# A two-layer hybrid decoder: layer A's memory projection behind four more value pieces, one gate block moved into its attention, one value tile in another PSUM bank, and the variances of the norms given priority

## The chip, the cores and the metric

The kernel runs on one core of one Trainium2 chip. The metric is the device time of one execution in microseconds (us). TensorE (PE) does the matrix products, VectorE (DVE) and ScalarE (ACT) the elementwise work, GpSimd (POOL) a few small powers, and SyncE (SP) issues nearly all DMAs. Each engine works through its own instructions in a fixed order and waits on semaphores for the others.

## The reference

512 tokens of width 1024 go through two layers. Layer A mixes with a chunked spatial gating beside an attention over 256 memory rows; layer B mixes with a forgetting attention beside a memory attention. Each layer ends in a SiLU feed-forward of width 2816.

```python
def reference(x, mem, ...):
    h = x
    for layer in range(DEPTH):                                   # 2
        a = rmsnorm(h, ln_mix_pre[layer])
        mem_n = rmsnorm(mem, ln_mem[layer])
        if layer < N_A_LAYERS:                                   # layer A
            proj = a @ w_in_a[layer]
            u, v, q_mem = proj[..., :768], proj[..., 768:1536], proj[..., 1536:]
            main = chunked_spatial_gating(u, v, ...)             # gelu(u) * (tril(w_s) @ layernorm(gelu(v)) + b_s)
        else:                                                    # layer B
            ...
            main = forgetting_attention(q, k_s, v_s, log_f_s)
        mixed = jnp.concatenate([main, memory_attention(q_mem, mem_n, w_mem_kv[layer])], axis=-1)
        h = h + rmsnorm(mixed @ w_out[layer], ln_mix_post[layer])
        f = rmsnorm(h, ln_ffn_pre[layer])
        f = (jax.nn.silu(f @ w_ffn_gate[layer]) * (f @ w_ffn_up[layer])) @ w_ffn_down[layer]
        h = h + rmsnorm(f, ln_ffn_post[layer])
    return h
```

## The kernel before

**Products in parts.** Every fp32 operand is cut in two parts: ScalarE rounds it to `hi` (a CAST at L241, or an ACTIVATE with a gain at L245), VectorE takes `lo` as what is left (L241, L246). `mm3` (L193 to L195) makes one product of three matmuls, hi by hi, lo by hi and hi by lo. Weights arrive by DMA in 128x1024 pieces (`raw`, four buffers in turn) and are cut into 128x512 pairs (`whi`, `wlo`, eight buffers), so a piece of weights can't be cut before an older pair was used for the last time.

**Order.** The code is written in one sequence. The framework's scheduler then sets the order on each engine from that sequence, the dependences and priorities; `tc.high_priority()` raises what is written under it. PSUM has three `mm`, three `lg` and two `tr` banks.

**Layer A, in the order written (`layer_a`).** The two query blocks are computed into one `mm` and one `lg` bank (`outs`) while the tokens arrive. Then come *value blocks* 0 to 2 (`value_block`): each is 8 *pieces* of 12 matmuls (128x256 out); two pieces fill one tile `v` for 128 tokens, which ScalarE evacuates into `vg`, scaled by the norm's factor `r4` (L617). The list `fill` holds the 24 pieces, and `pieces(n)` issues the next n. Between them stand:

- the norm of the tokens, `pre` (class `Norm`): `finish` sums squares over partitions with 1-wide matmuls into `st` (L290), adds eps on VectorE into `var` (L292), and takes the power -1/2 on GpSimd into `r` (L262); `spread` transposes `r` into a bank `rb` (L259) and copies it to `rbc` (L305). All scaled evacuations wait for that.
- the norm of the memory, with the same steps, into `rmem`; the parts `mparts` of the memory rows (`mem_inputs`); the cut of the key weights (`mem_key_weights`); and then `mem_project`: two key tiles of 24 matmuls (named `ps`) and two value tiles (`memv`).

Eight pieces are issued ahead of `mem_project`. The memory attention (`attend`, four heads) then has four pieces in each head. After it stand the gelus of `vg` (L663), the LayerNorm statistics, and the *gate blocks* (`gate_inputs`, 24 matmuls 128x512 each, named `ps`): three of them, then the spatial products `s` (L717) by turns with the other three, then the output projection.

**The other norms.** `Norm.finish` is used by the norm at each of three boundaries too (`boundary`, class `PairNorm`): into the feed-forward of layer A, into layer B, and into the feed-forward of layer B, twice each, for the two halves of the tokens. There residuals `h` (L826), squares `sq` (L317, L320) and parts `xslo` stand around it on VectorE.

Of the kernel before, what the change touches and what calls it, by code (L numbers as in the profile page):

```python
# [15 lines left out]
P = 128  # L16
T = 512
D = 1024
KT = 8
TB = T // P  # L20
NMEM = 256
# [5 lines left out]
RMS_EPS = 1e-6  # L27
# [13 lines left out]
def hybrid(ctx: ExitStack, tc: tile.TileContext, i: dict, out: bass.AP):  # L41
# [28 lines left out]
    def small(s, n=4, dt=F32):  # L70
        return sp.tile([P, n], dt, tag=f"s{n}", name=name(s))

    def ps(tag, shape=(P, T), s="ps"):
        return pp.tile(list(shape), F32, tag=tag, name=name(s), bufs=2 if tag == "tr" else 3)

    V, A, PE, G = nc.vector, nc.scalar, nc.tensor, nc.gpsimd
# [24 lines left out]
    def gain(block, k):  # L101
        c = block * KT + k
        return gains[:, c : c + 1]
# [5 lines left out]
                    fill=0.0, base=0, channel_multiplier=-1)  # L109
# [3 lines left out]
                    fill=0.0, base=0, channel_multiplier=-1)  # L113
# [6 lines left out]
                    fill=NEG, base=0, channel_multiplier=1)  # L120
# [28 lines left out]
    def prepared(src, shape, eng=None):  # L149

        raw = wp.tile([P, 1024], F32, tag="raw", name=name("raw"), bufs=4)
        n = shape[0] * shape[1]
        dst = raw[:, :n].rearrange("p (a b) -> p a b", a=src.shape[1]) if len(src.shape) == 3 else raw[:, :n]
        last_load[0] = nc.sync.dma_start(dst, src)
        return weight_parts(raw, shape, eng)

    def weight_parts(raw, shape, eng=None):
        n = shape[0] * shape[1]
        parts = []
        for d in range(0, n, 512):  # L160
            pair = pair_of_parts(min(512, n - d))
            split(raw[:, d : min(d + 512, n)], *pair, eng)
            parts += cut(pair, shape[1])
        return parts
# [26 lines left out]
    def mm3(o, w, x, start, stop, more=False):  # L191

        PE.matmul(o, w[0], x[0], start=start, stop=False, skip_group_check=more)  # L193
        PE.matmul(o, w[0], x[1], start=False, stop=False, skip_group_check=more)  # L194
        return PE.matmul(o, w[1], x[0], start=False, stop=stop, skip_group_check=more)  # L195
# [20 lines left out]
    def queue(blocks):  # L216

        fs, loads = [], {}
        for load, some in blocks:
            loads.setdefault(max(len(fs) - 3, 0), []).append(load)  # L220
            fs += some

        def run(n):
            for f in (*loads.get(n, ()), fs[n]):
                f()

        return [lambda n=n: run(n) for n in range(len(fs))]

    def take(pieces, n):
        some = pieces[:n]  # L230
        del pieces[:n]
        return some
# [10 lines left out]
    def scaled_parts(src, g, hi, lo):  # L243

        last_parts[:] = (A.activation(hi, src, AF.Copy, scale=g),  # L245
                         V.scalar_tensor_tensor(out=lo, in0=src, scalar=g, in1=hi, op0=ALU.mult, op1=ALU.subtract))  # L246
# [14 lines left out]
    def rsqrt(dst, src, n):  # L261
        G.tensor_tensor(out=dst, in0=src, in1=mhalf[:, :n], op=ALU.pow)  # L262

    class Norm:
# [16 lines left out]
        def finish(self, cols):  # L281

            c0, c1 = cols
            tbs = range(c0 // P, c1 // P)
            t0, t1 = c0 // P, c1 // P
            st = ps("tr", (P, 4), s="st")
            for tb in tbs:
                some = self.sums(tb, cols)
                for n, sq in enumerate(some):
                    PE.matmul(st[:, tb : tb + 1], sq, avg, start=n == 0, stop=n == len(some) - 1)  # L290
            v = small("var")
            V.tensor_scalar_add(v[:, t0:t1], st[:, t0:t1], RMS_EPS)  # L292
            rsqrt(self.r4[:, t0:t1], v[:, t0:t1], t1 - t0)

        def sums(self, tb, cols):
            return [self.acc[:, c + tb * P : c + (tb + 1) * P] for c in range(0, T, self.width)]
# [32 lines left out]
    rbc = cp.tile([P, T], F32, name="rbc")  # L329
# [5 lines left out]
    def parts(s):  # L335
        return [(act(f"{s}hi"), act(f"{s}lo")) for _ in range(KT)]
# [6 lines left out]
    def load_mem():  # L343
        tiles = [plain("mem", (P, 2, NMEM)) for _ in range(KT // 2)]
        for k2, t in enumerate(tiles):
            nc.sync.dma_start(t, i["mem"][:, 2 * k2 : 2 * k2 + 2, :])
        return tiles

    def mem_sums(memt):
        norm = Norm(NMEM)  # L350
        for t in memt:
            norm.add(t.rearrange("p a b -> p (a b)"))
        return norm
# [13 lines left out]
    def mem_key_weights(layer):  # L367
        return [prepared(i["w_mem_k"][layer, m], (KT, P)) for m in range(2)]

    def mem_inputs(layer, memt):  # L370
        xs = []
        for k in range(KT):
            t = act("mparts", shape=(P, 2, NMEM))
            scaled_parts(memt[k // 2][:, k % 2, :], gain(G_MEM + layer, k), t[:, 0, :], t[:, 1, :])
            xs.append((t[:, 0, :], t[:, 1, :]))
        return xs
# [188 lines left out]
    def layer_a():  # L565
        a = parts("a")
# [25 lines left out]
        vg, evacs = {}, []  # L592

        def value_block(j):

            w, o = [], []

            def load():
                for kh in range(2):
                    w.extend(prepared(i["w_a_v"][j, kh], (4, 256)))  # L600

            def piece(tk, kh):
                if kh == 0:
                    o.append(ps("mm", (P, 256), s="v"))
                c = slice(tk * P, (tk + 1) * P)
                for k in range(4 * kh, 4 * kh + 4):
                    mm3(o[tk], (a[k][0][:, c], a[k][1][:, c]), w[k], k == 0, k == KT - 1)
                if kh:
                    evacs.append(lambda: evacuate(tk))
                if pre.done:  # L610
                    while evacs:
                        evacs.pop(0)()

            def evacuate(tk):
                if tk % 2 == 0:
                    vg[j, tk // 2] = plain("vg", (P, 2, 256))
                A.activation(vg[j, tk // 2][:, tk % 2, :], o[tk], AF.Copy, scale=pre.r4[:, tk : tk + 1])  # L617

            return load, [lambda tk=tk, kh=kh: piece(tk, kh) for tk in range(TB) for kh in range(2)]

        with tc.tile_pool(name="sgu", bufs=1) as lp:
            bsp = lp.tile([P, NG, P], F32, name="bsp")
            fill = queue([value_block(j) for j in range(3)])
            outs = [ps(t) for t in ("mm", "lg")]
            for k in range(KT):
                for o, w in zip(outs, wq):
# [3 lines left out]
            def pieces(n):  # L630
                for f in take(fill, n):
                    f()
# [6 lines left out]
            pre.finish(FULL)  # L639
            pre.done = True  # L640
            memt = load_mem()
            pieces(1)
            pre.spread(FULL, rbc)
            qf = [plain("q") for _ in range(2)]
            for f, o in zip(qf, outs):
                V.scalar_tensor_tensor(out=f, in0=o, scalar=0.125, in1=rbc, op0=ALU.mult, op1=ALU.mult)
            norm = mem_sums(memt)
            pieces(1)
            xs = mem_inputs(0, memt)
            wk = mem_key_weights(0)  # L650
            norm.finish((0, NMEM))
            pieces(3)
            norm.spread((0, NMEM), rmem)
            V.tensor_copy(r4m, norm.r4[:, :2])
            q = [(act("q"), act("q")) for _ in range(2)]
# [3 lines left out]
            mixed = [None] * KT  # L659
            attend(mem_heads(0, q, mixed), between={n: take(fill, c) for n, c in enumerate((4, 4, 4, 4))})  # L660
            with tc.issue_after(last_exp[0].ins):
                for vt in vg.values():
                    A.activation(vt, vt, AF.Gelu_apprx_tanh)  # L663
            vrows = lp.tile([2 * NG, P], F32, name="vrows")
            vcols = lp.tile([P, 2 * NG], F32, name="vcols")
# [1 line left out]
                   for n, x in enumerate(("ln_v_g", "ln_v_b"))])  # L667
# [3 lines left out]
            G.affine_select(out=wsf[:, :MAIN].rearrange("p (a b) -> p a b", a=NG),  # L671
                            in_=wsf[:, :MAIN].rearrange("p (a b) -> p a b", a=NG), pattern=[[0, NG], [1, P]],
                            compare_op=ALU.is_ge, fill=0.0, base=0, channel_multiplier=-1)
            us, vp = [], {}
            mv = lp.tile([P, TB, 2], F32, name="mv")
            rv = small("rv")

            wu = []

            def gate_inputs(m):  # L680
                while len(wu) < min(m + 2, NG):
                    wu.append(prepared(i["w_a_u"][len(wu)], (KT, P)))
                [o] = group([wu[m]], a, FULL, ["mm"])
                us.append(plain("u"))
                V.tensor_mul(us[m], o, rbc)
                A.activation(us[m], us[m], AF.Gelu_apprx_tanh)

            def stats():
                for tk in range(TB):
                    st = sp.tile([P, 3, 6], F32, tag="bn", name=name("bn"))  # L690
                    for j in range(3):
                        V.bn_stats(out=st[:, j, :], in_=vg[j, tk // 2][:, tk % 2, :])
                    V.bn_aggr(out=mv[:, tk, :], in_=st)
                V.tensor_scalar_add(rv, mv[:, :, 1], LN_EPS)
                rsqrt(rv, rv, 4)
# [25 lines left out]
                V.tensor_mul(t2, t.rearrange("p a b -> p (a b)"), us[g])  # L721
                store(t2, mixed, g)

            gate_inputs(0)
            stats()
            ws = weight_parts(wsf, (NG, P))
            gate_inputs(1)
# [2 lines left out]
            o = ps("tr", (P, 2 * NG), s="vcols")  # L730
# [3 lines left out]
            for n in range(2):  # L734
                o = ps("lg", (P, 384), s="rows")
# [575 lines left out]


    phase = layer_a()

    def memory():
# [93 lines left out]
```

## Time and profile before

| | |
|---|---|
| median of 3 runs | 1122.04 us (1121.86 to 1122.38) |
| the profiled execution: its time | 1121.42 us |
| the profiled execution: its span | 1119.7 us |
| granted TensorE clock, mean | 0.999 |
| instructions | 19536 |
| PE busy | 99% of the span |
| DVE busy | 80% |
| ACT busy | 59% |
| POOL busy | 3% |

The span runs from the first instruction to the end of the last; the time holds some 1.7 us more. Matmuls are pipelined and the profile models their ends, so a matmul of 128x256 is listed with 0.28 us although the next one starts 0.12 us later; what PE loses is read from the distance between starts. In a timeline row stand the start, the busy time, the engine, the line, what is written and read, a count, and in brackets the idle time before it with what ended it. A row of waits gives the total, the number and the longest.

### The profile page before, as it was taken

To read this page: it belongs to the slowest core of one execution; us is meant where nothing else is said; L and a number is where in the kernel's file an instruction comes from. 1 tells how busy PE (TensorE), PEld (TensorE's weight loads), DVE (VectorE), ACT (ScalarE), POOL (GpSimd) and SP (SyncE) were. 2 spreads that over 40 slices of the span, in tenths; PEclk is the share of its full clock that TensorE was granted. 3 is DMA by queue.
4 is the path that set the end of the run, shared out by engine and by line. 5 is a ranking of instruction groups with operands and counts; after the bars stand their busy time and mean duration, and the time that the engine had idled before them with its cause. 6 is when DMAs were issued, how large, how long until landed. Compare 5 with 4: busy or idle time off the path is not lost.

```text
span 1119.7 us, 19536 instructions
## 1 busy us (share of the span) xinstructions
PE 1107.3 (99%) x7409; PEld 1002.7 (90%) x7409; DVE 892.0 (80%) x1721; ACT 660.3 (59%) x1388; POOL 28.5 (3%) x41
## 2 busy tenths in 40 slices
PE   8999999999999999999999999999999999999998
PEld 6998889999899899998988898889999899899996
DVE  7979448999598578796968889958998598588776
ACT  7775458755266255476757677768765266255453
POOL 0100001000000000001000000001000000000000
PEclk9999999999999999999999999999999999999999
DMA  7413231334224234244242655421235234233222
GB/s 265 151 49 109 77 97 58 100 108 151 76 89 140 74 99 127 76 135 148 63 128 59 153 128 137 135 76 57 65 106 152 74 101 133 70 109 118 76 76 76
DMA packets 63557, 118.12 MB, mean 105 GB/s; under 512 B 5164, under 2 KB 39992, under 8 KB 63464
## 3 DMA queue, kind: packets, MB, share of 16 engines
q1 hardware_dynamic: 62584, 116.05, 33.8%
q8 instruction: 58, 0.95, 0.4%
q0 software_dynamic: 192, 0.52, 0.2%
q10 hardware_dynamic: 688, 0.31, 0.1%
q14 instruction: 35, 0.29, 0.1%
HBM read 104.71 MB, written 2.10 MB: 95 GB/s over the span
## 4 chain that ended last, share of the span: by engine, by line
PE 86%; DVE 7%; ACT 3%; issue 2%; POOL 1%; DMA 1%; SPq 0%; POOLq 0%; DVEq 0%; ACTq 0%
PE y L193 9%; PE y L195 9%; PE y L194 9%; PE a L194 5%; PE a L193 5%; PE a L195 5%; PE ps L195 3%; PE ps L194 3%; PE ps L193 3%; PE e L193 3%; PE e L194 3%; PE x L194 3%; PE x L193 3%; PE x L195 3%; PE e L195 3%; DVE wlo L241 2%
## 5 line engine op out<-in xcount | busy, mean ns | idle before, releaser
L241 ACT CAST whi<-raw 128x512 fp32r<-128x512 f32 x460 | 276.2, 620 | 267.0 <-PE y L195 118.6
L241 DVE TENSOR_TENSOR wlo<-raw,whi 128x512 fp32r<-128x512 f32 x460 | 305.2, 685 | 108.8 <-ACT whi L241 106.6
L193 PE MATMUL y<-whi,fhi 128*128 128x512 f32 (+1 forms) x356 | 140.0, 394 | 0.0
L194 PE MATMUL y<-wlo,fhi 128*128 128x512 f32 (+1 forms) x356 | 139.4, 392 | 0.0
L195 PE MATMUL y<-whi,flo 128*128 128x512 f32 (+1 forms) x356 | 139.4, 392 | 0.0
L194 PE MATMUL a<-xslo,whi 128*128 128x256 f32 x320 | 90.0, 281 | 0.0
L194 PE MATMUL x<-xslo,whi 128*128 128x256 f32 x320 | 89.9, 281 | 0.0
L195 PE MATMUL x<-xshi,wlo 128*128 128x256 f32 x320 | 89.9, 281 | 0.0
L193 PE MATMUL x<-xshi,whi 128*128 128x256 f32 x320 | 89.8, 281 | 0.0
L193 PE MATMUL a<-xshi,whi 128*128 128x256 f32 x320 | 89.8, 281 | 0.0
L195 PE MATMUL a<-xshi,wlo 128*128 128x256 f32 x320 | 89.8, 281 | 0.0
L193 PEld LDWEIGHTS y<-whi,fhi 128*128 128x128 f32 x356 | 66.9, 188 | 15.7 <-ACT fhi L241 0.7
L195 PEld LDWEIGHTS y<-whi,flo 128*128 128x128 f32 x356 | 66.9, 188 | 15.5 <-DVE flo L241 0.2
L194 PEld LDWEIGHTS y<-wlo,fhi 128*128 128x128 f32 x356 | 67.0, 188 | 14.7 <-DVE wlo L241 0.2
L193 PE MATMUL ps<-xshi,whi 128*128 128x256 f32 (+1 forms) x224 | 67.5, 304 | 0.0
L195 PE MATMUL ps<-xshi,wlo 128*128 128x256 f32 (+1 forms) x224 | 67.1, 302 | 0.1
L194 PE MATMUL ps<-xslo,whi 128*128 128x256 f32 (+1 forms) x224 | 66.4, 299 | 0.0
L193 PEld LDWEIGHTS a<-xshi,whi 128*128 128x128 f32 x320 | 60.4, 189 | 0.4
L194 PEld LDWEIGHTS a<-xslo,whi 128*128 128x128 f32 x320 | 60.3, 188 | 0.3
L193 PEld LDWEIGHTS x<-xshi,whi 128*128 128x128 f32 x320 | 60.4, 189 | 0.0
L195 PEld LDWEIGHTS x<-xshi,wlo 128*128 128x128 f32 x320 | 60.3, 189 | 0.0
L194 PEld LDWEIGHTS x<-xslo,whi 128*128 128x128 f32 x320 | 60.3, 188 | 0.0
(283 smaller groups left out, 3091.1 us busy)
## 6 DMA issues: line engine op xcount, KB each, us to landing
raw<-in_w_gate SPq DMA_DIRECT2D x44, 512.0 KB, 3.6
raw<-in_w_up SPq DMA_DIRECT2D x44, 512.0 KB, 3.5
raw<-in_w_down SPq DMA_DIRECT2D x44, 512.0 KB, 4.0
raw<-in_w_out SPq DMA_DIRECT2D x16, 512.0 KB, 4.5
raw<-in_w_b_q SPq DMA_DIRECT2D x8, 512.0 KB, 3.5
raw<-in_w_a_v SPq DMA_DIRECT2D x6, 512.0 KB, 7.0
raw<-in_w_a_u SPq DMA_DIRECT2D x6, 512.0 KB
raw<-in_w_v SPq DMA_DIRECT2D x6, 512.0 KB, 3.7
```

The costliest lines, as they stand in the source:

```text
L193: PE.matmul(o, w[0], x[0], start=start, stop=False, skip_group_check=more)
L194: PE.matmul(o, w[0], x[1], start=False, stop=False, skip_group_check=more)
L195: return PE.matmul(o, w[1], x[0], start=False, stop=stop, skip_group_check=more)
L241: last_parts[:] = A.copy(hi, src), (eng or V).tensor_sub(lo, src, hi)
```

## The change

Five edits, all in layer A's code but the first:

1. `Norm.finish` puts the eps addition and the power under `tc.high_priority()`, so for every norm in the kernel.
2. The third value tile, for (j, tk) = (0, 2), goes into an `lg` bank, not an `mm` bank.
3. Twelve pieces of the value blocks are issued ahead of the memory projection, not eight: `pieces` has 1, 2, 2, 2, 5 in place of 1, 2, 1, 1, 3. The memory norm's `finish` is written ahead of the cut of the key weights.
4. Gate block 0 becomes part of `fill` behind the value blocks (`gate_block`, four pieces of six matmuls). The attention's four heads still take four pieces each: the last 12 value pieces, and then gate block 0.
5. Its gelu joins those of `vg`, and `gate_inputs(0)` after the attention goes away.

```diff
             v = small("var")
-            V.tensor_scalar_add(v[:, t0:t1], st[:, t0:t1], RMS_EPS)
-            rsqrt(self.r4[:, t0:t1], v[:, t0:t1], t1 - t0)
+            with tc.high_priority():
+                V.tensor_scalar_add(v[:, t0:t1], st[:, t0:t1], RMS_EPS)
+                rsqrt(self.r4[:, t0:t1], v[:, t0:t1], t1 - t0)
...
                 if kh == 0:
-                    o.append(ps("mm", (P, 256), s="v"))
+                    o.append(ps("lg" if (j, tk) == (0, 2) else "mm", (P, 256), s="v"))
...
-            fill = queue([value_block(j) for j in range(3)])
+            us, wu = [], []
+
+            def gate_block(m):
+                o = []
+                def load():
+                    wu.append(prepared(i["w_a_u"][m], (KT, P)))
+                def piece(n):
+                    if n == 0:
+                        o.append(ps("mm", s="u"))
+                    for k in range(2 * n, 2 * n + 2):
+                        mm3(o[0], wu[m][k], a[k], k == 0, k == KT - 1)
+                    if n == 3:
+                        us.append(plain("u"))
+                        V.tensor_mul(us[m], o[0], rbc)
+                return load, [lambda n=n: piece(n) for n in range(4)]
+
+            fill = queue([value_block(j) for j in range(3)] + [gate_block(0)])
...
             memt = load_mem()
-            pieces(1)
+            pieces(2)
             pre.spread(FULL, rbc)
...
             norm = mem_sums(memt)
-            pieces(1)
+            pieces(2)
             xs = mem_inputs(0, memt)
+            norm.finish((0, NMEM))
             wk = mem_key_weights(0)
-            norm.finish((0, NMEM))
-            pieces(3)
+            pieces(5)
             norm.spread((0, NMEM), rmem)
...
             with tc.issue_after(last_exp[0].ins):
-                for vt in vg.values():
+                for vt in (*vg.values(), us[0]):
                     A.activation(vt, vt, AF.Gelu_apprx_tanh)
...
-            gate_inputs(0)
             stats()
             ws = weight_parts(wsf, (NG, P))
             gate_inputs(1)
```

What this does to the order of the instructions is seen at three places. (Eighteen lines are added ahead of most of the code, so line numbers are a little higher in the changed kernel.)

VectorE, layer A, behind the variance of the tokens' norm (`var`). Before:

```order
L292 TENSOR_SCALAR var_323<-st_318 128x4
L279 TENSOR_TENSOR acc_360<-acc_360,sq_368 128x512
L246 SCALAR_TENSOR_TENSOR mparts_384<-mem_326,gains,mparts_384 128x256
L246 SCALAR_TENSOR_TENSOR mparts_387<-mem_326,gains,mparts_387 128x256
L305 COPY rbc<-rb_349 128x512
```

And in the changed kernel, where raw_384 and raw_394 are the weights of value block 1:

```order
L293 TENSOR_SCALAR var_323<-st_318 128x4
L279 TENSOR_TENSOR acc_373<-acc_373,sq_381 128x512
L241 TENSOR_TENSOR wlo_387<-raw_384,whi_386 128x512
L241 TENSOR_TENSOR wlo_391<-raw_384,whi_390 128x512
L241 TENSOR_TENSOR wlo_397<-raw_394,whi_396 128x512
L241 TENSOR_TENSOR wlo_401<-raw_394,whi_400 128x512
L306 COPY rbc<-rb_362 128x512
```

The variance stands where it stood; behind it, four subtractions of weights come ahead of the memory's parts.

TensorE, layer A, around the transposes of the memory norm (`rb`; `ps` are the key tiles, `v` a value tile). Before:

```order
L193 MATMUL ps_533<-mparts_393,whi_410 128x256
L194 MATMUL ps_533<-mparts_393,whi_410 128x256
L195 MATMUL ps_533<-mparts_393,wlo_411 128x256
L259 MATMUL rb_496<-ident,r_2_359 128x128 x2
L193 MATMUL ps_533<-mparts_396,whi_414 128x256
```

And in the changed kernel:

```order
L193 MATMUL v_523<-whi_400,ahi_132 128x256
L194 MATMUL v_523<-wlo_401,ahi_132 128x256
L195 MATMUL v_523<-whi_400,alo_133 128x256
L259 MATMUL rb_549<-ident,r_2_372 128x128 x2
L193 MATMUL ps_586<-mparts_431,whi_465 128x256
```

Between the sums `st` of that norm and these transposes stood 48 matmuls of 128x256; now 60 stand there, all of them of value tiles. For the tokens' norm there were 10 between its `st` and its `rb`, and now 22.

VectorE, the boundary into the feed-forward of layer A, first half of the tokens. Before:

```order
L826 SCALAR_TENSOR_TENSOR h<-yt_2180,gains,h 128x256
L320 TENSOR_TENSOR sq_2120<-sq_2120,sq_2177 128x512
L241 TENSOR_TENSOR xslo_2174<-hs_2170,xshi_2173 128x512
L826 SCALAR_TENSOR_TENSOR h<-yt_2180,gains,h 128x256
L292 TENSOR_SCALAR var_2213<-st_2210 128x2
L931 TENSOR_TENSOR hs_1937<-hs_1937,hs_2113 128x512
L305 COPY rbc<-rb_2228 128x256
```

And in the changed kernel:

```order
L293 TENSOR_SCALAR var_2213<-st_2210 128x2
L844 SCALAR_TENSOR_TENSOR h<-yt_2180,gains,h 128x256
L321 TENSOR_TENSOR sq_2120<-sq_2120,sq_2177 128x512
L241 TENSOR_TENSOR xslo_2174<-hs_2170,xshi_2173 128x512
L844 SCALAR_TENSOR_TENSOR h<-yt_2180,gains,h 128x256
L306 COPY rbc<-rb_2228 128x256
```

The variance moves up by four instructions. On TensorE the transposes `rb` move up with it, from 23 matmuls behind `st` to 12. The boundary into the feed-forward of layer B changes in the same way, and at the one into layer B the distance goes from 24 matmuls to 10.

More of the change, by code (lines that the diff above doesn't have):

```diff
@@ L673, in layer_a @@
                             compare_op=ALU.is_ge, fill=0.0, base=0, channel_multiplier=-1)
-            us, vp = [], {}
+            vp = {}
             mv = lp.tile([P, TB, 2], F32, name="mv")
             rv = small("rv")
-            wu = []
             def gate_inputs(m):
```

## The prediction

> **What bounds the kernel now.** I read the page's head first, then the waits by engine, then the timeline around each wait of PE.
>
> ```profile
> span 1119.7 us, 19536 instructions
> PE 1107.3 (99%) x7409; PEld 1002.7 (90%) x7409; DVE 892.0 (80%) x1721; ACT 660.3 (59%) x1388; POOL 28.5 (3%) x41
> ```
>
> PE is busy for 99% of the span, and the change neither adds nor removes a matmul. So only two things can move the time: gaps of PE that go, and gaps that come. The waits of PE in layer A up to 170 us:
>
> ```profile
> PE rb L259 <- POOL r L262: 2.2, 2, 1.7
> PE tr L456 <- DVE mp L449: 0.3, 1, 0.3
> PE mo L485 <- ACT pT L241: 0.2, 1, 0.2
> ```
>
> These list idle time after the modelled end of a matmul; the true loss is the distance between starts less the nominal one. The timeline gives both `rb` waits, and the boundary into layer A's feed-forward has a smaller one:
>
> ```profile
> 25.29 0.16 DVE L292 TENSOR_SCALAR var<-st 128x4 f32<-128x4 f32 x1 [1.57 <-PE st L290]
> 25.37 0.69 DVE L279 TENSOR_TENSOR acc<-acc,sq 128x512 f32<-128x512 f32 x1
> 25.53 1.41 POOL L262 TENSOR_TENSOR r<-var,mhalf 128x4 f32<-128x4 f32 x1 [22.60 <-DVE var L292]
> 25.98 0.87 DVE L246 SCALAR_TENSOR_TENSOR mparts<-mem,gains,mparts 128x256 fp32r<-128x256 f32 x2
> 26.24 0.28 PE L195 MATMUL v<-whi,alo 128*128 128x256 f32 x1
> 26.99 0.65 PE L259 MATMUL rb<-ident,r 128*128 128x128 f32 x4 [0.47 <-POOL r L262]
> ...
> 29.02 0.95 PE L290 MATMUL st<-avg,acc 128*128 128x1 f32 x8
> 34.27 0.15 DVE L292 TENSOR_SCALAR var<-st 128x2 f32<-128x2 f32 x1
> 34.34 2.48 DVE L241 TENSOR_TENSOR wlo<-raw,whi 128x512 fp32r<-128x512 f32 x4
> 34.49 2.89 POOL L262 TENSOR_TENSOR r<-var,mhalf 128x2 f32<-128x2 f32 x1 [7.56 <-DVE var L292]
> 35.44 0.28 PE L195 MATMUL ps<-mparts,wlo 128*128 128x256 f32 x1
> 37.44 0.43 PE L259 MATMUL rb<-ident,r 128*128 128x128 f32 x2 [1.73 <-POOL r L262]
> ...
> 53.69 0.28 PE L194 MATMUL v<-wlo,ahi 128*128 128x256 f32 x1
> 54.01 0.62 DVE L449 TENSOR_SCALAR mp<-mp,sm 128x256 f32<-128x256 f32 x2
> 54.16 0.28 PE L195 MATMUL v<-whi,alo 128*128 128x256 f32 x1
> 54.77 0.63 PE L456 MATMUL tr<-ident,mp 128*128 128x128 f32 x4 [0.33 <-DVE mp L449]
> ...
> 184.72 0.50 PE L290 MATMUL st<-avg,sq 128*128 128x1 f32 x4
> 184.82 0.48 DVE L826 SCALAR_TENSOR_TENSOR h<-yt,gains,h 128x256 f32<-128x256 f32 x1
> 185.26 0.69 DVE L320 TENSOR_TENSOR sq<-sq,sq 128x512 f32<-128x512 f32 x1
> 186.86 0.15 DVE L292 TENSOR_SCALAR var<-st 128x2 f32<-128x2 f32 x1
> 186.93 0.68 DVE L931 TENSOR_TENSOR hs<-hs,hs 128x512 f32<-128x512 f32 x1
> 187.18 0.98 POOL L262 TENSOR_TENSOR r<-var,mhalf 128x2 f32<-128x2 f32 x1 [11.82 <-DVE var L292]
> 187.76 0.28 PE L194 MATMUL ps<-xslo,whi 128*128 128x256 f32 x1
> 188.22 0.43 PE L259 MATMUL rb<-ident,r 128*128 128x128 f32 x2 [0.18 <-POOL r L262]
> ```
>
> From 53.69 to 54.16 are four steps of `v`, so one 128x256 matmul costs 0.117 us. With that the losses are: tokens' norm 26.99 − 26.24 − 0.117 = 0.63; memory norm 37.44 − 35.44 − 0.117 = 1.89; `tr` 54.77 − 54.16 − 0.117 = 0.49; boundary 188.22 − 187.76 − 0.117 = 0.34. I allow the same 0.34 for the boundary into layer B's feed-forward, which the change treats alike (an estimate).
>
> Two things make POOL late. The memory's variance starts at 34.27 although its sums ended before 30: VectorE's order put it there. And the power itself takes 0.98 to 2.89 us. What it takes when left alone, and in a worse place, the next rows show.
>
> ```profile
> 166.22 0.87 DVE L826 SCALAR_TENSOR_TENSOR h<-yt,gains,h 128x256 f32<-128x256 f32 x2
> 166.38 0.54 POOL L262 TENSOR_TENSOR r<-v,mhalf 128x1 f32<-128x1 f32 x1 [4.99 <-DVE v L795]
> ...
> 555.38 2.49 DVE L241 TENSOR_TENSOR wlo<-raw,whi 128x512 fp32r<-128x512 f32 x4
> 555.54 1.08 POOL L262 TENSOR_TENSOR r<-var,mhalf 128x2 f32<-128x2 f32 x1 [5.38 <-DVE var L292]
> ```
>
> Beside `h`, which reads PSUM, the power takes 0.54. Beside VectorE's two-operand SBUF instructions it ends about 0.55 after one of them ends: 188.16 against 187.61 for `hs`; 37.38 against 36.82 for the four `wlo`. At 555.54 it came in after the first of four, at 34.49 after the last. So the power seems to be kept out while such an instruction runs, and where it comes in is not fixed.
>
> **The change part by part.**
>
> *Memory norm.* 60 matmuls now stand between `st` and `rb`, not 48, so the last of them starts 12 x 0.117 = 1.40 later, near 36.8 on before's clock. More matters that the variance is written ahead of the key weights and raised: in the new order it stands ahead of VectorE's four `wlo`, so `r` loses at most what it loses now (2.89) from a start near 32 to 33, and is there by 36. I take the whole wait as gone: −1.89. Ends: −1.89 and 0.
>
> *Tokens' norm.* The variance stands at the same row of VectorE's order, so the priority does nothing. But behind it now come `acc` and four `wlo`, all with two SBUF operands, up to about 26.06 + 4 x 0.62 = 28.54. PE reaches `rb` 12 matmuls later, at 26.36 + 1.40 = 27.76. If the power is kept out as at 34.49, it ends near 28.4 to 29.1, a wait of 0.7 to 1.4; if it comes in after `acc` or the first `wlo` (as at 555.54), at 26.6 to 27.3, no wait. I take the lower value of the first, as 34.49 has the same four in a row: +0.1 against the 0.63 of now. Ends: −0.63 and +0.75.
>
> *Third value tile in another bank.* The fourth tile needs a bank that the first one's evacuation frees, which follows `r` at once, and PE has 12 matmuls (1.4 us) before it. Nothing: 0. The split weights of value block 1 are now needed some 12 us earlier; their transfers take what is now the key weights' place on the queue:
>
> ```profile
> 11.41 1.58 SPq L154 DMA_DIRECT2D raw<-in_w_mem_k  x2
> 16.34 2.13 SPq L154 DMA_DIRECT2D raw<-in_w_a_v  x2
> 20.00:30.00 10.00, 9.53 (x81) 9.23 (x81) 7.38 (x15) 7.04 (x17) 1.41 (x1) 1.00 0.21 81
> ```
>
> (The last row is a window: PE, PEld, DVE, ACT and POOL busy, clock, DMA share, GB/s.) They land near 13, and the key weights near 18.5; by the order VectorE cuts the first only behind the variance of 25.29, and the others later still. The four extra cuts cost VectorE 4 x 0.62 = 2.5 us in a stretch where it is busy for 7.4 of 10. All 0.
>
> *First heads.* The wait of `tr` comes from VectorE's `mp` being late by 0.5. VectorE leaves the memory projection earlier, since its cuts are done ahead; against that gate block 0's weights are cut inside the attention. −0.49; ends −0.49 and +0.5. The fourth pair of weights of the memory's values must wait for the key products to free its buffer, with a margin of 0.1 to 0.2 by my count: +0.1, ends 0 and +0.5.
>
> *End of attention to the first spatial product.* Here the change takes cover away.
>
> ```profile
> 76.60 0.28 PE L474 MATMUL mlg<-memk,q 128*128 128x256 f32 x1
> 94.45 0.68 DVE L241 TENSOR_TENSOR vlo<-vg,vhi 128x512 fp32r<-128x512 f32 x1
> 100.67 0.27 PE L193 MATMUL s<-whi,vhi 128*128 128x128 f32 x1
> 80.00:100.00 20.00, 19.84 (x93) 15.70 (x92) 19.10 (x47) 15.44 (x29) 1.31 (x1) 1.00 0.24 80
> ```
>
> From the last logits to the first `s` are 24.07 us. By the order 24 matmuls of 128x256 and 12 of 128x512 fewer stand there; the wide ones are twice as long (an estimate, 0.235), so the cover falls by 2.81 + 2.82 = 5.6 to 18.4. The chain of exponentials, gelus, statistics, `vg` and `vlo` has its second `vlo`, which the first `s` group needs last, ready at 95.13, that is 18.53 after the logits; PE needs it some 0.7 after that group begins. It fits with about 0.6 to spare, and VectorE has one `u` and two weight cuts less in that stretch: 0; ends −0.2 (the `mo` wait) and +1.5 (VectorE is busy for 19.1 of 20 us there, so nothing can catch up).
>
> *Boundaries.* The variance moves up by four instructions, the transposes by 11 matmuls. PE reaches `rb` at 187.88 − 11 x 0.117 = 186.59. VectorE waits for `st` (last one started near 185.0) and runs `var` at about 185.26, then `h`, whose second operand is in PSUM, and then `sq`. POOL begins near 185.55, beside `h`; as at 166.38 it takes 0.54 and ends at 186.1, ahead of PE. Both waits go: −0.34 x 2 = −0.68, of which I give back 0.1 for the 0.4 that VectorE now waits. If instead `sq` and `xslo` keep it out, it ends near 187.5, a wait of 0.9, 0.55 more each. I take the first, as the neighbour is the same instruction as at 166.38. Ends −0.68 and +1.1 for the two. Layer B's boundary shows no wait now: 0, ends 0 and +0.6.
>
> The Trainium skill, "SBUF — State Buffer", section "SBUF: two separate sides", says that VectorE and GpSimd share a port pair as an exclusive lock: whichever begins first, GpSimd's instruction or a VectorE one of the fast mode or with two SBUF operands, holds it to its end. That agrees with 34.49 and 187.18; no row here shows a VectorE instruction that had to wait for POOL. By it the power at the boundary, begun beside `h`, goes first and `sq` waits, as in my sum; without it the sum would be by the second case.
>
> **The sum.** −1.89 + 0.1 − 0.49 + 0.1 − 0.58 = −2.76. The profiled execution took 1121.42 (the span and 1.7 around it), so 1118.7 by it; the median of the three runs is 0.62 above it, which gives 1119.3.
>
> **Rivals.**
>
> 1. *POOL is kept out at the boundaries too.* For it: 187.18 and 34.49, each behind such an instruction; `sq` follows `h` at 0.44, before the power can be done. Against: 166.38, with a second `h` following. Boundaries +1.1 in place of −0.58: sum −1.1, 1121.0.
> 2. *POOL slips in at the tokens' norm.* For it 555.54, against it 34.49. −0.63 in place of +0.1: sum −3.5, 1118.5.
> 3. *The waits in the attention stay or come back.* `tr` unchanged and 0.5 each at the memory's values and `mo`: sum −1.4, 1120.6. For it: VectorE is near full from 80 on; against: up to 60 the cuts that delayed it are done ahead.
> 4. *The cover taken away is too little, and the kernel is slower.* The chain to the first `s` runs on VectorE at 19.1 of 20; were it longer behind the logits by 0.6, each further us costs PE one. Slower by 2.24 needs the chain late by 2.8 + 2.2 + 0.6 = 5.6 us, the whole shift of cover, as if nothing of the chain followed the logits. For it only the full VectorE; against: the row at 94.45 stands 6 us ahead of 100.67. At that point 1124.3.
> 5. *The edit of the order doesn't do what it says:* at the tokens' norm that is certain; at the memory norm it would leave 1.89 of wait, 1121.2; against it stands the order.
>
> **How the numbers follow.** A measurement of this kernel tells some 0.2% (2.24 us) from no change. Chances: the forecast 0.40; rival 1 0.27; rival 2 0.14; rival 3 0.09; rival 4 0.06; rival 5 0.04. The likeliest gives 1119.3, with 1118.8 to 1119.9 as its own range. With rivals 1, 2, 3 and 5 the range reaches from 1118.0 (all lower ends) to 1121.5. Faster than 1119.8: the forecast for the most part (0.36), rival 2 (0.14), and a third of rival 3 (0.03), so 0.53. Slower: rival 4, 0.06. The rest, 0.41, is within 0.2%.
>
> **What would show it.** No wait of `rb` at the memory norm, `r` well ahead of it; at the tokens' norm a wait near 0.7 with POOL at 2.5 to 3; no wait of `tr`; the first `s` without one; POOL at 0.5 to 0.6 at the feed-forward boundaries. I am wrong if POOL there takes 1.5 or more, if PE shows a new wait between 39 and 100 us, or if `s` waits.

## The result, and the profile after

| | median (range) | ratio to before (95% interval) |
|---|---|---|
| before, beside it | 1121.96 us (1121.72 to 1122.38) | |
| changed | 1117.52 us (1116.10 to 1120.65) | 0.9964 (0.9951 to 0.9977) |
| before, a second time | 1121.35 us (1120.59 to 1122.94) | |
| changed, beside it | 1117.10 us (1116.88 to 1117.54) | 0.9961 (0.9948 to 0.9973) |

The kernel is faster by 4.4 us (0.4%), the second time by 4.25. The forecast was 1119.3 with a range of 1118.0 to 1121.5: the direction was right, the gain was larger than the whole range. The profiled execution took 1117.77.

The page's head and the waits of PE up to 170 us, of the changed kernel (total, times, longest):

```profile
span 1116.1 us, 19541 instructions
PE 1104.8 (99%) x7409; PEld 1001.5 (90%) x7409; DVE 891.3 (80%) x1721; ACT 660.2 (59%) x1388; POOL 24.6 (2%) x41
...
PE idle L88 <- DVE zeros L80: 1.3, 1, 1.3
PE ps L193 <- ACT ahi L245: 0.5, 1, 0.5
PE ps L194 <- DVE alo L246: 0.3, 1, 0.3
```

All three rows that were shown of before (`rb`, `tr`, `mo`) are gone from this list, though `mo` still loses 0.23 between starts; what is left is the start-up, where before waits too. The timeline at the tokens' norm, the memory norm, the first `s` and the boundary into layer A's feed-forward:

```profile
25.07 0.16 DVE L293 TENSOR_SCALAR var<-st 128x4 f32<-128x4 f32 x1 [1.09 <-PE st L290]
25.16 0.69 DVE L279 TENSOR_TENSOR acc<-acc,sq 128x512 f32<-128x512 f32 x1
25.32 1.41 POOL L262 TENSOR_TENSOR r<-var,mhalf 128x4 f32<-128x4 f32 x1 [22.39 <-DVE var L293]
25.76 1.89 DVE L241 TENSOR_TENSOR wlo<-raw,whi 128x512 fp32r<-128x512 f32 x3
27.57 0.60 PE L259 MATMUL rb<-ident,r 128*128 128x128 f32 x4
...
31.82 0.16 DVE L293 TENSOR_SCALAR var<-st 128x2 f32<-128x2 f32 x1 [0.40 <-PE st L290]
31.91 2.46 DVE L246 SCALAR_TENSOR_TENSOR mparts<-mem,gains,mparts 128x256 fp32r<-128x256 f32 x6
32.05 0.90 POOL L262 TENSOR_TENSOR r<-var,mhalf 128x2 f32<-128x2 f32 x1 [5.32 <-DVE var L293]
38.79 0.38 PE L259 MATMUL rb<-ident,r 128*128 128x128 f32 x2
...
78.56 0.28 PE L474 MATMUL mlg<-memk,q 128*128 128x256 f32 x1
96.98 0.28 PE L193 MATMUL s<-whi,vhi 128*128 128x128 f32 x1
...
181.47 0.16 DVE L293 TENSOR_SCALAR var<-st 128x2 f32<-128x2 f32 x1 [0.35 <-PE st L290]
181.80 0.70 POOL L262 TENSOR_TENSOR r<-var,mhalf 128x2 f32<-128x2 f32 x1 [10.21 <-DVE var L293]
181.94 0.68 DVE L321 TENSOR_TENSOR sq<-sq,sq 128x512 f32<-128x512 f32 x1
182.78 0.38 PE L259 MATMUL rb<-ident,r 128*128 128x128 f32 x2
```

None of the three `rb` rows has a bracket: PE came to them without waiting. The power was done 0.84 us ahead of PE at the tokens' norm (26.73 against 27.57), 5.8 us at the memory norm and 0.28 us at the boundary. From the last logits to the first `s` are 18.4 us, the cover that the forecast counted, and `s` does not wait.

One wait is new, in layer B's feed-forward. ScalarE stands for the down weights, VectorE's `s` comes behind their cuts, and PE stands for `s`. First the two casts of before, then the changed kernel:

```profile
856.12 1.14 ACT L241 CAST whi<-raw 128x512 fp32r<-128x512 f32 x2 [1.91 <-DMA raw<-in_w_down]
857.68 1.15 ACT L241 CAST whi<-raw 128x512 fp32r<-128x512 f32 x2 [0.42 <-DMA raw<-in_w_down]
...
850.66 1.14 ACT L241 CAST whi<-raw 128x512 fp32r<-128x512 f32 x2 [2.12 <-DMA raw<-in_w_down]
853.88 1.14 ACT L241 CAST whi<-raw 128x512 fp32r<-128x512 f32 x2 [2.08 <-DMA raw<-in_w_down]
854.06 0.40 PE L195 MATMUL y<-whi,flo 128*128 128x512 f32 x1
856.22 0.50 PE L193 MATMUL y<-whi,fhi 128*128 128x512 f32 x1 [1.76 <-DVE s L1027]
```

From start to start of PE are 2.16 us where 0.23 is a step: 1.92 lost in this execution. The second cast comes 3.22 us behind the first, where before has 1.56.

### The profile page after: what moved, and what is told of

The parts are those of the page before. It is cut to its first block, busy times and chain, and to the rows that moved or that the text cites. A ratio compares the mean times of both kernels' runs of the same rounds, so it can differ in the third digit from the quotient of the medians.

```text
span 1116.1 us, 19541 instructions
## 1 busy us (share of the span) xinstructions
PE 1104.8 (99%) x7409; PEld 1001.5 (90%) x7409; DVE 891.3 (80%) x1721; ACT 660.2 (59%) x1388; POOL 24.6 (2%) x41
## 4 chain that ended last, share of the span: by engine, by line
PE 84%; DVE 8%; ACT 3%; DMA 2%; issue 2%; POOL 0%; SPq 0%; POOLq 0%; DVEq 0%; ACTq 0%
PE y L193 9%; PE y L194 9%; PE y L195 9%; PE a L195 4%; PE a L193 4%; PE a L194 4%; PE ps L195 4%; PE ps L193 4%; PE ps L194 4%; PE x L195 3%; PE x L193 3%; PE x L194 3%; PE e L193 3%; PE e L195 3%; PE e L194 3%; DVE wlo L241 3%
```

## The experiments

Each kernel is compared with runs of the kernel before on the same chip, whose medians were 1121.73 us for the priority alone, the kernel without the priority, the finish alone and the gate block; 1121.43 for the copy among the cuts and the three that vary the pieces and the bank; and 1121.35 for the addition among the cuts, the changed kernel once more and the loads issued by GpSimd. The intervals are 0.1% or so to each side, over 1 us, so what single waits do is read from the distances between PE's starts, and the times say whether the sum is right.

**The priority alone**, on the kernel before:

```diff
+            with tc.high_priority():
                 V.tensor_scalar_add(v[:, t0:t1], st[:, t0:t1], RMS_EPS)
                 rsqrt(self.r4[:, t0:t1], v[:, t0:t1], t1 - t0)
```

> The kernel before with the priority in Norm.finish alone. Theory (the gain is the sum of single waits of PE that go): the memory norm's variance moves ahead of the key weights' cuts in VectorE's order, so the rb wait of 1.9 us goes, though PE then stands closer behind the cuts of the key weights (0 to 0.5 us may come back there); the two boundary waits of 0.34 and 0.32 go; the wait at the tokens' norm (0.63) and that of tr (0.49) stay. Time 2.0 to 2.6 us under before, about 1119.6. Rival (the twelve pieces ahead of the memory projection are what takes the memory norm's wait away, and the variance's place matters little): only the boundaries gain, 0.7 us, about 1121.3.

1120.55, that is 1.2 us under before (0.9989, 0.998 to 0.9998), between the theory and the rival. The memory norm's wait and those of the boundaries went, but another came. PE and VectorE in the memory projection:

```profile
39.91 0.28 PE L193 MATMUL memv<-whi,mparts 128*128 128x256 f32 x1
40.75 2.50 DVE L241 TENSOR_TENSOR wlo<-raw,whi 128x512 fp32r<-128x512 f32 x4
41.50 0.39 PE L194 MATMUL memv<-wlo,mparts 128*128 128x256 f32 x1 [1.31 <-DVE wlo L241]
```

PE now stands before the memory's value weights, whose first cut ends after 41.4: 1.48 us lost (41.50 − 39.91 − 0.117), where before had lost 0.11. Of the 1.89 only 0.4 is kept. My 0 to 0.5 for this was too small, and it was put at the key weights; it is the value weights behind them that are late.

**The changed kernel without the priority.**

> The changed kernel without the priority. Theory: VectorE's order in layer A puts the memory norm's variance ahead of the key weights all the same, because its finish is written there, so all of layer A's gain stays and only the two boundary waits come back: 0.65 us over the changed kernel, about 1118.2. Rival (the raised variance is what gives the gain in layer A too): the wait of 1.9 us at the memory norm's rb comes back as well, about 1120.1.

1117.99, 3.7 us under before (0.9968, 0.9955 to 0.998). No wait at the memory norm; both boundary waits are back, 0.31 and 0.34. So in layer A the priority isn't needed, and at the boundaries it is worth 0.65.

**The memory norm's finish ahead of the key weights, alone**, on the kernel before:

```diff
-            wk = mem_key_weights(0)
             norm.finish((0, NMEM))
+            wk = mem_key_weights(0)
```

> The kernel before with the memory norm's finish written ahead of the cut of the key weights, and nothing else. Theory: PE's wait at the memory norm's rb goes (1.9 us), up to 0.5 of it may come back as a wait for the key weights' cuts; tokens' norm, tr and boundaries as before: 1120.0 to 1120.6. Rival (pieces, not the place of the variance): no more than 0.3 us under before.

1124.79, slower by 3.1 us (1.0024, 1.0014 to 1.0034). Both theories failed. The variance moved from 34.27 to 31.84 as meant, and the power came no earlier:

```profile
31.84 0.15 DVE L292 TENSOR_SCALAR var<-st 128x2 f32<-128x2 f32 x1
31.91 4.90 DVE L241 TENSOR_TENSOR wlo<-raw,whi 128x512 fp32r<-128x512 f32 x8
32.08 5.30 POOL L262 TENSOR_TENSOR r<-var,mhalf 128x2 f32<-128x2 f32 x1 [5.15 <-DVE var L292]
37.43 0.54 PE L259 MATMUL rb<-ident,r 128*128 128x128 f32 x2 [3.11 <-POOL r L262]
```

Eight cuts stand behind the variance in one row, and the power is kept out until the last ends: 5.30 us, as it was 2.89 behind four. PE reaches `rb` 12 matmuls sooner, since they now stand behind it, and loses 3.27. Windows of the same kernel (bounds, length, PE, PEld, DVE, ACT and POOL busy, granted clock, DMA share, GB/s) show a second loss:

```profile
34.00:37.40 3.40, 0.32 (x3) 0.12 (x1) 2.81 (x5) 3.34 (x7) 3.37 (x1) 1.00 0.90 265
37.40:41.00 3.60, 3.57 (x18) 3.58 (x19) 2.88 (x6) 0.63 (x2) 0.00 (x0) 0.53 0.97 370
```

Behind the wait the granted clock is 0.53 for 3.6 us, and 18 matmuls start where before has 30 in the same window.

**The same, with one copy of 128x1 among the eight cuts:**

```diff
             norm.finish((0, NMEM))
-            wk = mem_key_weights(0)
+            wk = [prepared(i["w_mem_k"][0, 0], (KT, P))]
+            gap = small("gap", 1)
+            V.tensor_copy(gap, wk[0][KT - 1][1][:, :1])
+            wk.append(prepared(i["w_mem_k"][0, 1], (KT, P)))
```

> The kernel with the finish ahead of the key weights alone, and one more VectorE instruction, a copy of 128x1, behind the third of the eight cuts that kept the power out for 5.30 us. Theory (the power gets in only where the row of two-operand SBUF instructions is broken): it ends 0.56 us behind the third cut, near 34.3, after 2.3 instead of 5.3 us; the rb wait falls from 3.27 to 0.2 or 0.3 us, and a wait for the memory's value weights of up to 1.5 us takes its place: 1.5 to 3 us under the kernel without the copy. Rival (such a copy is no break): 5.3 us and 3.27 us again.

1121.44, level with before (0.9997, 0.9987 to 1.0006) and some 3.1 under the kernel without the copy, each against its own runs of before:

```profile
31.89 1.88 DVE L241 TENSOR_TENSOR wlo<-raw,whi 128x512 fp32r<-128x512 f32 x3
32.05 2.29 POOL L262 TENSOR_TENSOR r<-var,mhalf 128x2 f32<-128x2 f32 x1 [5.15 <-DVE var L292]
33.69 0.15 DVE L653 COPY gap<-wlo 128x1 f32<-128x1 f32 x1
33.75 3.09 DVE L241 TENSOR_TENSOR wlo<-raw,whi 128x512 fp32r<-128x512 f32 x5
34.39 0.43 PE L259 MATMUL rb<-ident,r 128*128 128x128 f32 x2
```

The power gets in behind the third cut and ends 0.57 after it (34.34 against 33.77). PE loses 0.30 at `rb` and 0.43 at the memory's values, the latter less than I had allowed. By PE's starts this kernel is 1.1 us ahead of before behind layer A's attention; its profile loses 1.19 at the down weights (0.1 in before), and the times are level.

**The same, with an addition of two 128x1 operands in place of the copy** (`V.tensor_tensor(out=gap, in0=whi column, in1=wlo column, op=ALU.add)`):

> As the kernel with the copy of 128x1 behind the third of eight cuts, but with an addition of two SBUF operands of 128x1 in place of the copy. Theory A (any instruction of another shape between the cuts lets the power in): 2.3 us as with the copy, and a wait of 0.3 us at rb. Theory B (only an instruction with one SBUF operand lets it in): 5.3 to 5.4 us, and a wait of 3.3 us.

1121.61 (1.0001, 0.9991 to 1.0011). The power took 2.30 us and PE lost 0.29: theory A, for this place: both small instructions let the power in, so the number of SBUF operands is not what does it here. That another shape is enough is not shown. In the kernel before a power was kept out through a cut of 128x512 and a smaller one behind it (128x256), and ended 0.56 after the second, when an instruction with an operand in PSUM followed:

```profile
194.05 0.68 DVE L241 TENSOR_TENSOR wlo<-raw,whi 128x512 fp32r<-128x512 f32 x1
194.20 1.42 POOL L262 TENSOR_TENSOR r<-var,mhalf 128x2 f32<-128x2 f32 x1 [6.04 <-DVE var L292]
194.65 0.41 DVE L241 TENSOR_TENSOR flo<-f,fhi 128x256 fp32r<-128x256 f32 x1
```

The small instructions also read what the cuts ahead of them write; whether their size or such a dependence makes the opening was not tested.

**The changed kernel with gate block 0 back behind the attention** (three value pieces in each head):

> The changed kernel with gate block 0 back behind the attention, so that each head has three value pieces (36 matmuls) instead of four. Theory (gate block 0 only replaces the four value pieces that went ahead of the memory projection): the heads have 12 matmuls (1.4 us) less to hide the softmax chains, so the tr and mo waits grow by 0.5 to 1.5 us each over four heads: 1 to 4 us over the changed kernel, 1118.5 to 1121.5; the tokens' norm, memory norm and boundaries stay without waits. Rival (the heads have cover to spare): the same time as the changed kernel within 0.5 us. On the scatter of the changed kernel's runs (1116.1 to 1120.65): if the late transfer of down weights seen at 854 us comes by chance, kernels of this call scatter alike, the kernel before included; if it comes with an earlier PE, only those that are faster scatter.

1118.10, 3.6 us under before (0.9971, 0.996 to 0.9983). No wait of `tr`, and 0.37 at `mo` where the changed kernel has 0.23. The rival held: the heads have cover to spare, and moving the gate block is worth 0.1 to 0.2 us in the waits of layer A, less than the times can tell. The question about the scatter stays open: before spread over 3.0 us in 20 runs, this kernel over 3.5 in six, the priority alone over 1.1 in eleven.

**The twelve pieces and the `lg` bank alone**, on the kernel before:

```diff
-                    o.append(ps("mm", (P, 256), s="v"))
+                    o.append(ps("lg" if (j, tk) == (0, 2) else "mm", (P, 256), s="v"))
...
             memt = load_mem()
-            pieces(1)
+            pieces(2)
...
             norm = mem_sums(memt)
-            pieces(1)
+            pieces(2)
...
             norm.finish((0, NMEM))
-            pieces(3)
+            pieces(5)
...
-            attend(mem_heads(0, q, mixed), between={n: take(fill, c) for n, c in enumerate((4, 4, 4, 4))})
+            attend(mem_heads(0, q, mixed), between={n: take(fill, c) for n, c in enumerate((3, 3, 3, 3))})
```

> The kernel before with only the twelve pieces ahead of the memory projection and the third value tile in an lg bank (three pieces in each head); no priority, the memory norm's finish where it was, gate block 0 behind the attention. Theory (the twelve pieces alone carry layer A's gain: they give the memory norm's power and the cuts of the memory's weights 1.4 us more each): no wait at the tokens' norm, the memory norm, the memory's values or tr; only the boundary waits (0.65 us) stay: 3.4 to 4.0 us under before. Rival (the place of the variance is needed as well): VectorE has the variance behind the four cuts of the key weights, so the power starts near 36.9 and is kept out by the next two-operand work until 40: a wait of 1.0 to 1.5 us at the memory norm's rb, 2.2 to 2.8 under before.

1118.66, 2.8 us under before (0.9976, 0.9967 to 0.9985), less than the 3.4 to 4.0 of the theory. In its profile every wait of layer A is gone but `mo` (0.38), and the boundaries keep theirs (0.36 and 0.38), as the theory has it. The rival's wait did not come, since the row of two-operand work is broken by a copy (`r4m`) that itself waits for the power:

```profile
36.15 0.16 DVE L292 TENSOR_SCALAR var<-st 128x2 f32<-128x2 f32 x1
36.34 0.69 DVE L365 TENSOR_TENSOR q<-q,q 64x512 fp32r<-64x512 f32 x1
36.39 1.20 POOL L262 TENSOR_TENSOR r<-var,mhalf 128x2 f32<-128x2 f32 x1 [9.62 <-DVE var L292]
37.62 0.17 DVE L654 COPY r4m<-r 128x2 f32<-128x2 f32 x1 [0.60 <-POOL r L262]
```

The profiled execution (1120.92) lost 2.81 us at the down weights near 857; how much of that is in the other ten runs isn't known.

**The changed kernel with eight pieces ahead of the memory projection** (1, 2, 1, 1, 3, and five in each head):

> The changed kernel with eight pieces ahead of the memory projection, as before (five pieces in each head, gate block 0 among them); priority, finish and gate block as changed. Theory: as with the priority alone, the rb wait of the memory norm goes but PE then stands in front of the memory's value weights, whose cuts VectorE has not done: a wait of 1.3 to 1.6 us at memv; the tokens' norm waits 0.63 as before, the boundaries not at all: 1.2 to 2.0 us under before. Rival (priority and finish do it): 3 us or more under before.

1120.44, 1.0 us under before (0.9991, 0.9983 to 1.0). Of its waits of PE up to 60 us those behind the start-up:

```profile
PE memv L194 <- DVE wlo L241: 1.3, 1, 1.3
...
PE rb L259 <- POOL r L262: 0.5, 1, 0.5
...
PE tr L457 <- DVE mp L450: 0.2, 1, 0.2
```

The memory's values cost 1.47 and the tokens' norm 0.63, as expected, `tr` still 0.41, and the time lies just outside the expected 1.2 to 2.0. Priority, finish and gate block without the four pieces are worth about 1 us.

**The changed kernel with the third value tile in an `mm` bank:**

> The changed kernel with the third value tile in an mm bank again. Theory: that tile then can't begin before ScalarE has evacuated the first one, which needs the tokens' norm's power: the wait of 0.6 to 0.8 us of before comes back there, as a wait of v, and nothing else changes: 0.6 to 0.9 us over the changed kernel, 3.5 to 3.9 under before. Rival (the wait has gone for another reason, such as a faster power): no difference to the changed kernel.

1119.07, 2.4 us under before (0.9975, 0.9964 to 0.9986).

```profile
25.39 0.28 PE L195 MATMUL v<-whi,alo 128*128 128x256 f32 x1
26.14 0.43 PE L259 MATMUL rb<-ident,r 128*128 128x128 f32 x2 [0.47 <-POOL r L262]
26.65 0.39 PE L193 MATMUL v<-whi,ahi 128*128 128x256 f32 x1
```

Two transposes now stand ahead of the tile, and PE loses 0.63 at them and 0.24 behind: 0.87. Without a free bank PE cannot use the twelve matmuls that were to cover the power. The power itself took 1.41 in this kernel too. By the times it gains some 2 us less than the changed kernel, each against its own runs of before; the rows account for 0.9 of that.

**The changed kernel once more:**

> The changed kernel once more, beside the next two. Theory (single waits of PE, and one transfer that lands late by chance): tokens' norm with a power of 1.41 us and no wait, memory norm 0.90 and no wait, boundaries 0.70 and no wait, in the profile as in the first one; the wait for the down weights near 856 us differs from profile to profile (0 to 2.8 us in the ten so far). 3.5 to 4.5 us under before. Rival (the gain over the forecast was a lucky set of runs): 2.8 us under before.

1117.10, 4.25 under before, with powers of 1.41, 0.90 and 0.70 and no wait at any of them. The gain over the forecast was no luck of one set of runs.

**The changed kernel with the down weights' loads issued by GpSimd** (`nc.gpsimd.dma_start` in place of `nc.sync.dma_start`):

> The changed kernel with the loads of the down weights issued by GpSimd, not SyncE. Theory (the load that lands late near 856 us is held up behind the other loads of SyncE's queue, where its issue takes 0.4 to 1.2 us): the wait for it goes, 0.5 to 2 us under the changed kernel, with less scatter. Rival (GpSimd's issue is slower, and is kept out by VectorE as its powers are): new waits for down weights all through the two feed-forwards, slower than the changed kernel by 3 us or more.

1118.78, 2.6 us under before (0.9978, 0.9967 to 0.9989), 1.7 over the changed kernel beside it. Neither held: PE still lost 0.54 near 856, and 0.70 more at 269, where it had lost nothing. Taking the loads off SyncE's queue did not take the loss away, so that queue alone doesn't explain it; 0.54 is within what the profiles scatter by.

## Why the prediction was right or wrong

What each term measured, by PE's starts in the two first profiles:

| term | forecast | measured |
|---|---|---|
| memory norm | −1.89 | −1.89 |
| tokens' norm | +0.1 | −0.63, and −0.17 in the transposes and the step behind them |
| `tr` in the first head | −0.49 | −0.49 |
| memory's values | +0.1 | −0.11 |
| `mo`, end of the attention | 0 | −0.10 |
| first `s` | 0 | 0 |
| boundaries | −0.58 | −0.66 |
| sum | −2.76 | −4.05 |
| steps of layer A's feed-forward | none | −0.86 |
| `e` in it, near 266 us | none | +0.20 |
| down weights near 856 us | none | +1.8 in this profile |

*Tokens' norm: the first step that failed.* The prediction took the power to be kept out by the four `wlo` behind the variance, "as 34.49 has the same four in a row". But `acc` stands between, and the power came in behind `acc`: it ended 0.88 after it (26.73 against 25.85), exactly as in before (26.94 against 26.06), where other work followed. The row that was quoted, 25.53 with 1.41, said this already: I read it as a mild case of being kept out, and it was the undisturbed end of one instruction and a power on four columns. With the wait at 0, the sum would have been −3.5, which was rival 2, at 0.14. That alone is 0.73 of the 1.29 by which the terms were off. 0.17 more lies behind the wait: from the start of `rb` to the second matmul behind it before takes 0.73 us (26.99 to 27.72) and the changed kernel 0.56 (27.57 to 28.13), nearly all of it in the four transposes. I counted no such time for any of the waits.

*"Only two things can move the time", gaps that go and gaps that come: the second step that failed.* Between two points of layer A's feed-forward, the `e` behind a wait and the first `yt`, stand the same 1764 matmuls in both kernels, with no wait among them and the granted clock at 1.00. Before, then the changed kernel:

```profile
266.44 0.39 PE L193 MATMUL e<-t,whi 128*128 128x256 f32 x1 [0.42 <-ACT s L1003]
527.22 0.60 PE L821 MATMUL yt<-ident,y 128*128 128x128 f32 x4
...
262.00 0.39 PE L193 MATMUL e<-t,whi 128*128 128x256 f32 x1 [0.61 <-ACT s L1021]
521.93 0.49 PE L839 MATMUL yt<-ident,y 128*128 128x128 f32 x3
```

That is 260.78 us against 259.92, 0.86 less, with a mean step of 118.2 ns against 117.8 for the 128x256 matmuls. It is no scatter: the changed kernel once more takes 259.90, without the priority 259.90 and with the third tile in an `mm` bank 259.89; the priority alone, the finish alone and the two with an instruction among the cuts take 260.78 or 260.79; the pieces alone, eight pieces and the gate block behind the attention 260.16 to 260.26. So a change of layer A's order can move the pace of matmuls far behind it, and the prediction had nothing for that. What sets the pace stays open.

*Third value tile: costed at nothing, right for the tile and incomplete for the change.* The bank is what lets PE reach the twelve matmuls ahead of `rb`; the run without it loses 0.87 there. The prediction also took the ends of the rows that issue the loads, 13 and 18.5, for landings: the load issued at 16.34 landed 5.3 us later, near 21.7. PE waited for none of these weights, so the 0 stands.

*Memory norm: right in size, and incomplete in its reason.* I gave the variance's place as what matters more. The runs say that the place is worth little by itself: brought forward by priority it trades 1.89 for 1.48 at the memory's values, brought forward by the finish it makes the wait longer. The four pieces take the wait away without it (the pieces alone, and the run without the priority, where the variance stands ahead of four cuts and the power still takes 2.89). They give 1.4 us to the power and to VectorE's cuts alike, so that the next thing to be late isn't late either.

*Memory's values: wrong sign.* I feared for the buffers of the fourth pair of weights; what decided in the runs with the priority alone and with eight pieces is how far VectorE's cuts lag behind PE there, and in the changed kernel PE comes 1.4 us later. The 0.11 of before, a slow step without idle time, went; why isn't shown.

*Boundaries, `tr`, cover ahead of `s`: right.* The power starts beside `h` and ends 0.28 us ahead of PE. Its length was 0.70, not the 0.54 I used, which was one column's. The Trainium skill, "SBUF — State Buffer", section "SBUF: two separate sides", has GpSimd's instruction hold the shared ports to its end once it has begun first, and the other block. Half of it is seen here: the power that began at 181.80 beside `h` ran its undisturbed 0.70 although `sq` began at 181.94. The other half is not: `sq` took its usual 0.68, and in the run with the copy five cuts took 3.09 us from 33.75 on, 0.60 each as in the uninterrupted row of eight, while the power ran until 34.34. No VectorE instruction was seen to be held up by a power.

*The range.* All its lower ends add up to −3.89, that is 1118.15, put at 1118.0, and the median lay 0.5 below that. The terms and the pace of the feed-forward give 4.7 net of `e`, where the times have 4.4; against them stands the late load. A closer sum isn't possible: in the start-up, which the change leaves alone, the changed kernel's two profiles were already 0.2 and 0.7 us ahead of that of before.

*The late load of down weights.* In thirteen profiles it cost between nothing (the priority alone) and 2.8 us (the pieces alone), 0.1 in before, 1.9 and 1.1 in the two of the changed kernel. The finish alone and the two with an instruction among the cuts have none of the twelve pieces and lost 0.7 to 1.2, so it doesn't take the change to bring it; whether before is spared in its other runs isn't known. Why a 512 KB load issued in the same place lands later stays open. It is the likeliest source of the changed kernel's wide first range (1116.10 to 1120.65), but runs without a profile don't show it.

## What to carry to other kernels

When PE is the bound, a wait that is taken away only pays if the next input is early too: work put ahead of the waiting point moves everything behind it back and covers several late inputs at once, while an earlier producer only moves the wait on. Before giving an instruction on GpSimd an earlier place, look at what VectorE runs behind its input: rows of four and of eight equal 128x512 cuts kept it out to their end here, and a 128x1 instruction among them let it in. Check this in the profile of your own kernel, since other rows of two-operand instructions let the power in after the first. A bank that is still occupied takes away the cover that the order promises. And compare the pace of stretches without waits too: 0.86 of the gain here lies in one.

## What the runs showed of the hardware

*The power and VectorE.* Behind an unbroken row of `wlo` (128x512, two SBUF operands) the power of 128x2 ended 0.56 to 0.57 us after the row's last instruction: 2.89 us for four, 5.30 for eight, and 2.29 and 2.30 where a 128x1 instruction stood behind the third. Undisturbed it took 0.70. What breaks a row isn't settled: at layer B's boundary it came in after the first of four equal cuts (1.08), in before and in the changed kernel alike; at the changed kernel's memory norm after the first of six `mparts` (0.90), which have two SBUF operands as well; behind `acc` although `wlo` followed; and at 194.20 in before a smaller cut did not let it in.

*The clock after a wait.* After PE had lost 3.27 us the granted clock was 0.53 for 3.6 us, and with eight pieces, after a loss of 2.60 us at the down weights, 0.52:

```profile
860.60:863.60 3.00, 2.93 (x7) 2.36 (x8) 2.44 (x6) 1.28 (x3) 0.00 (x0) 0.52 0.62 192
```

After 2.81 us in the run of the pieces alone it stayed at 1.00, as it did after the 1.89 of before. The Trainium skill, "TensorE: Matmul & The Clock Gate", section "What's actually happening", puts the return to half rate after an idle window of some 3.4 us that runs free of the kernel. The half rate agrees; the window does not, since both waits are shorter than it, and here the measurement decides: a wait of 2.6 us can be long enough. The phase may explain why 2.60 was enough and 2.81 was not, but no run here tells that. In the kernel with the finish alone the half rate cost 1.5 us on top of the wait (sixteen matmuls at 0.213 instead of 0.117). Of its nine runs eight have a mean clock of 0.996 to 0.998; the one with 0.999 is the shortest, 1121.58.
